# A decoder trunk's attention units: the value products one unit later, on one Trainium2 core

## The chip, the cores and the metric

The kernel runs on one core of one Trainium2 chip. The metric is the device time of one execution in microseconds (us), lower is better. Engines are named as in the profile: PE multiplies matrices (PEld loads its weights), DVE, ACT and POOL work on vectors, SP issues most DMAs. Each engine takes its instructions in the order of its own queue and waits at the head of the queue for what the instruction needs.

## The reference, cut to what matters

```python
u = x * (1 + scale) + shift                  # x: (2048, 1024)
q, k, v, a_gate, p_in, p_gate, m_a, m_p = split(u @ w_in)
# 16 query heads of 64, 2 key heads; blocks of 128 queries see the 256 keys of their own
# block and of the one before, within a window of 128
logits = qb @ kb.T * 64 ** -0.5 + bias       # masked by window
probs = softmax(concat([logits, sink], -1))[..., :-1]
a = (probs @ vb) * silu(a_gate)
p = (pool(p_in) @ w_mix * pool_scale) * silu(p_gate)
y = (sigmoid(m_a) * (a @ w_attn_proj) + sigmoid(m_p) * (p @ w_pool_proj)) @ w_out * (1 + gate)
x = layer_norm(alpha * x + y)
```

All of it is computed in fp32 accuracy: a matrix product is three products of high and low parts (`mm3`), so operands are split into a rounded copy and a rest (`low`, a subtraction).

## The kernel before

The 2048 rows are worked on in two halves of 1024 (`s` = 0, 1). For each half there are two phases, the gates' ring and the attention, and a last phase mixes both halves.

**The gates' ring** (`gate_quads`, `ring`, `back`) computes keys, values, gates and the first four query tiles. It works through groups of two pairs of weight tiles (`Quad`); one group, the last but one, has a single pair. `back` multiplies the group in five products a pair; `ask` puts off the load of a pair of the next group (`load`, issued on SP) by one tick and its first sum on POOL (`sum1`) by three. A tick is one product of twelve matmuls. SP's loads there are not held in program order: the layer that records the program may place them elsewhere in SP's queue.

**The attention** (`attention`) runs 64 units in each half and a few more that drain it. Unit `n` stands for two heads and one block of 128 queries. Its steps are spread over several units, so that in the loop's pass `n` the engines work on the units `n`, `n-1`, `n-2` and `n-3`:

- scores of unit `n` on PE (`score_mms`: four matmuls, tile `lg`); on DVE the bias is added and the row's bound taken, one instruction for each head (tiles `L`, `nm`); on ACT the exponential with its row sum (`L`, `sm`), again one for each head;
- of unit `n-1` on DVE the reciprocal of the sums (`sm`), on ACT the scaling of the first head's `L` by it, on DVE that of the second head's (a `tensor_scalar`);
- of unit `n-2` on PE four transposes (`turn_mms`, tile `pt`), on ACT the rounded copy `pth`, on DVE the rest `ptl`, then on PE the four value products (`value_mms`, tile `pv`, from `pth` and `ptl`);
- of unit `n-3` on ACT the copy of the lower half of `pv` (`o2`, shown as `o<-pv`), and on DVE two additions of `o2` and the upper half of `pv` into `o` (shown as `o<-pv,o`).

`pt`, `pv`, `pth` and `ptl` have one buffer each; `lg` has two, `L` three. All engines' instructions of this loop, the value products included, are kept in the order in which they are written. In each pass PE also runs 9 or 12 matmuls of another projection (`project`, shown as `mm<-set_..`), and for some passes ACT and DVE have more to do at the end of the pass: they split a tile of queries (`take_q`, tile `qs`: two instructions on ACT, then two on DVE), ACT copies a pool input (`vb`), DVE ends a pool difference (`pool_diff`, tile `nxt`). POOL adds pool sums and multiplies by gates.

In the pass before the change the additions of `n-3` stand on DVE behind the reciprocal and ahead of the two bias instructions, and PE's value products of `n-2` stand last.

Of the kernel before, what the change touches and what calls it, by code (L numbers as in the profile page):

```python
# [12 lines left out]
F32 = mybir.dt.float32  # L13
F32R = mybir.dt.float32r
AF = mybir.ActivationFunctionType
ALU = mybir.AluOpType
# [3 lines left out]
P = 128  # L20
# [3 lines left out]
CH = 512  # L24
NCH = S // CH
NB = CH // P
HEADS = 16
HD = 64
# [31 lines left out]
def kernel(  # L60
# [22 lines left out]
    nc = tc.nc  # L83
# [48 lines left out]
    def low(engine, dst, src, hi):  # L132
        engine.tensor_tensor(dst, src, as32(hi), ALU.subtract)  # L133
# [228 lines left out]

    def back(ph, grp, opened, nxt, own, tick, b22_first=False):
        st = []
        for q, (a, b, c, w, *copy) in zip(grp, opened):
            p5 = ph.p("p5")
            if w is None:
                c = bank("lg")
                nc.scalar.copy(c, a)
                nc.scalar.copy(p5, b)  # L370
                w = pair_split(ph, q.second())[::-1]
                q.late()
                product(c, w[1], "T2")
            else:
                u2 = copy[0] if copy else ph.p("u2")
                if not copy:
                    nc.scalar.copy(u2, a)
                if c is None:
                    c = bank("lg")
                    product(c, w[1], "T2", True)  # L380
                nc.vector.tensor_tensor(c, c, u2, ALU.add)
                nc.scalar.copy(p5, b)
            tick()
            nc.vector.tensor_tensor(b, c, p5, ALU.add)
            if not copy:
                product(a, w[0], "B21")
            tick()
            q.consume(ph, 0, 0, a)
            st.append((q, b, c, p5))
        w = {}  # L390

        def ask(q):

            defer(1, lambda: q.load(ph, own, sp if b22_first else nc.sync, None))
            defer(3, lambda: q.sum1(nc.gpsimd))

        def third(x):
            w[x] = pair_split(ph, st[x][0].third())[::-1]
            if x < len(nxt):
                ask(nxt[x])  # L400

        def with_t3(x):
            q, b, c, p5 = st[x]
            product(c, w[x][1], "T3")
            tick()
            nc.vector.tensor_tensor(p5, c, p5, ALU.add)
            q.consume(ph, 1, 1, p5)

        def with_b22(x):
            q, b, c, p5 = st[x]  # L410
            product(b, w[x][0], "B22")
            tick()
            q.consume(ph, 0, 1, b)

        if b22_first:
            for x in range(len(st)):
                third(x)
                with_b22(x)
            for x in range(len(st)):
                with_t3(x)  # L420
        else:
            for x in range(len(st)):
                third(x)
                with_t3(x)
                with_b22(x)
        for q in nxt[len(st) :]:
            ask(q)
        for q, b, c, p5 in st:
            w = half_split(ph, q.a22)
            product(c, w, "T4")  # L430
            tick()
            q.consume(ph, 1, 0, c)
# [29 lines left out]
    def defer(ticks, f):  # L462
        due.append((now[0] + ticks, len(due), f))
# [272 lines left out]
    def attention(ph, s, q0, nxt):  # L736
# [91 lines left out]
        def score_mms(j, b, q, qs):  # L828
            k0 = P if s == 0 and b == 0 else 0
            lg = bank("lg").rearrange("p (h k) -> p h k", h=2)  # L830
            for h in range(2):
                for hl in range(2):
                    mm(
                        lg[:, h, k0:],
                        qs[:, h, q * P : (q + 1) * P],
                        kk[:, j // 4, hl, b * P + k0 : (b + 2) * P],
                        start=hl == 0,
                        stop=hl == 1,
                    )
# [46 lines left out]
        bts = {0: bias_tile(0)}  # L886
        raw_q = {}
        parts, accs, sums = {}, {}, {}
        lgs, exps, Ls, pvs, outs, ags, pgs = {}, {}, {}, {}, {}, {}, {}
        opened = []  # L890
        act.activation(warm, mhalf, AF.Exp)

# [32 lines left out]
        for n in range(N + 5):  # L925
# [1 line left out]
            if n == 0:  # L927
                project(n)
            if n < N:
                lgs[n] = score_mms(j, n % U, b, qs[j, t])  # L930
            pt = None
            if n - 2 in Ls:
                L, k0 = Ls.pop(n - 2)
                pt = turn_mms(L, k0)
            if n - 1 in exps:
                sm = exps[n - 1][2]
                dve.reciprocal(sm, sm)
            if n - 3 in pvs:
                pv = pvs.pop(n - 3)
                jj, tt, bb = (n - 3) // U, (n - 3) // NB % 2, (n - 3) % NB  # L940
                if bb == 0:
                    outs[jj, tt] = tp.tile([P, CH], F32, tag="o", bufs=2, name="o")
                if bb == 1:
                    ags[jj, tt] = ld("ag", gates_d["ag"][s, jj, tt])
                o2 = tp.tile([HD, 2, P], F32, tag="o2", bufs=2, name="o2")
                act.copy(o2, pv[HD:])
                for h in range(2):
                    dve.tensor_tensor(
                        outs[jj, tt][h * HD : (h + 1) * HD, bb * P : (bb + 1) * P], pv[0:HD, h, :], o2[:, h, :], ALU.add
                    )  # L950
            if n - 1 in exps:
                E, e0, sm = exps[n - 1]
                act.activation(E[:, 0, e0:256], E[:, 0, e0:256], AF.Copy, scale=sm[:, 0:1])
            if pt is not None:
                h0 = k0 // P
                pth = tp.tile([P, 2, 2, P], F32R, tag="pth", bufs=1, name="pth")
                ptl = tp.tile([P, 2, 2, P], F32R, tag="ptl", bufs=1, name="ptl")
                act.copy(pth[:, h0:], pt[:, h0:])
            if n < N:
                lg, c0 = lgs.pop(n)  # L960
                L = tp.tile([P, 2, 260], F32, tag="L", bufs=3, name="L")
                nm = tp.tile([P, 2], F32, tag="nm", bufs=4, name="nm")
                sm = tp.tile([P, 2], F32, tag="sm", bufs=4, name="sm")
                act.copy(L[:, :, 256], nsink[:, 2 * j : 2 * j + 2])
# [19 lines left out]
                exps[n] = (L, c0, sm)  # L984
            if pt is not None:
                low(dve, ptl[:, h0:], pt[:, h0:], pth[:, h0:])
            if n - 1 in exps:
                E, e0, sm = exps.pop(n - 1)
                dve.tensor_scalar(E[:, 1, e0:256], E[:, 1, e0:256], sm[:, 1:2], None, ALU.mult)
                Ls[n - 1] = (E, e0)  # L990
            if 0 < n < 60:
                project(n)
            elif n >= 60:
                fill_one(n)
            if pt is not None:
                pvs[n - 2] = value_mms((n - 2) // U, (n - 2) % U, k0, pth, ptl)


            for w in range(1, len(order)):
# [546 lines left out]
```

## Time and profile before

| what | us |
|---|---|
| median of 3 runs (lowest, highest) | 1816.47 (1813.97, 1816.5) |
| the profiled execution's own time | 1815.8 |
| its span, first to last instruction | 1814.0 |
| first attention, units 0 to 63 begin | 455 to 704 |
| second attention, units 0 to 63 begin | 1076 to 1331 |

The mean granted clock of PE is 0.986 of full speed. In rows of the timeline the first number is the start in us from the span's start, the second the duration in us; a bracket at the end gives the engine's idle time just before and what released it. All instructions of the attention stand at line 56 of the kernel, through which the ordered engines record, so they are told apart by tiles. `(x)` in a table of stretches is the count of instructions.

### The profile page before, as it was taken

The numbers are of one execution on the slowest core, as the hardware profiler recorded it, in microseconds if no ns is written. First come the engines' busy times: TensorE is split into PE (matmuls) and PEld (weight loads), VectorE is DVE, ScalarE is ACT, GpSimd is POOL, SyncE is SP. The second block draws the span as 40 slices with busy tenths as digits, with TensorE's granted clock in tenths as the row PEclk, the third lists the DMA queues.
The fourth block names the chain that finished last, engine by engine and source line by source line (L and its number), as shares of the span: only waits on it lengthen the run. The fifth ranks groups of instructions, "written<-read, shape, count | busy, mean of one in ns | idle before, by whom it ended". The sixth has DMA issues, their size and how long they took to land. (4 is left out here: it accounts for less than half of the span.)

```text
span 1814.0 us, 25046 instructions
## 1 busy us (share of the span) xinstructions
PE 1718.8 (95%) x8200; PEld 1426.4 (79%) x8200; DVE 1232.6 (68%) x2200; ACT 951.7 (52%) x1997; POOL 804.7 (44%) x628
## 2 busy tenths in 40 slices
PE   6899999999998998999999999899999999999997
PEld 5688878878777787888788888677888877888785
DVE  5977656434777887667755338878877675865777
ACT  4644444434877777545444447777854334423452
POOL 2154344521265557434424304644574662355542
PEclk9999999999999999999999999999999999999998
DMA  9375766762445447686776454534687675689432
GB/s 359 123 273 196 244 238 252 264 150 98 146 161 169 163 149 302 235 289 247 276 265 241 168 192 140 175 134 158 219 304 275 198 234 185 232 287 399 166 140 105
DMA packets 185010, 387.60 MB, mean 214 GB/s; under 512 B 19232, under 2 KB 39728, under 8 KB 184880
## 3 DMA queue, kind: packets, MB, share of 16 engines
q1 hardware_dynamic: 178240, 370.22, 58.8%
q0 software_dynamic: 3552, 11.56, 1.6%
q10 hardware_dynamic: 3088, 4.23, 0.8%
q8 instruction: 65, 1.06, 0.2%
q14 instruction: 65, 0.53, 0.1%
HBM read 247.49 MB, written 141.59 MB: 214 GB/s over the span
## 5 line engine op out<-in xcount | busy, mean ns | idle before, releaser
L56 PE MATMUL mm<-set_B,w_set 128*128 128x512 f32 x3024 | 757.2, 397 | 11.8 <-DVE w_set L133 7.0
L56 PEld LDWEIGHTS mm<-set_B,w_set 128*128 128x128 f32 x3024 | 567.3, 190 | 131.8 <-DVE w_set L133 9.6
L56 PE MATMUL lg<-set_T,w_set 128*128 128x512 f32 x2232 | 542.6, 394 | 18.6 <-DVE w_set L133 10.3
L56 PEld LDWEIGHTS lg<-set_T,w_set 128*128 128x128 f32 x2232 | 419.6, 189 | 114.7 <-DVE w_set L133 14.9
L133 DVE TENSOR_TENSOR w_set<-W,w_set 128x1024 fp32r<-128x1024 f32 x174 | 237.4, 1364 | 230.2 <-ACT w_set L326 214.9
L326 ACT CAST w_set<-W 128x1024 fp32r<-128x1024 f32 x174 | 182.5, 1049 | 282.1 <-PE mm L56 220.1
L56 PE MATMUL mm<-set_T,w_set 128*128 128x512 f32 x1008 | 252.7, 395 | 0.0
L56 PEld LDWEIGHTS mm<-set_T,w_set 128*128 128x128 f32 x1008 | 188.8, 190 | 38.9 <-DVE nxt L56 0.2
L295 POOL TENSOR_TENSOR W<-W,A 128x512 f32<-128x512 f32 x60 | 85.3, 1422 | 267.3 <-DMA W<-in_win_dram 65.1
L304 POOL TENSOR_TENSOR W<-W 128x512 f32<-128x512 f32 x60 | 84.3, 1406 | 187.9 <-DVE w_set L133 177.8
L299 POOL TENSOR_TENSOR W<-W 128x512 f32<-128x512 f32 x60 | 95.9, 1599 | 97.3 <-DVE w_set L133 88.2
L56 ACT ACTIVATE L<-L,nm 128x257 f32<-128x257 f32 (+1 forms) x256 | 127.0, 498 | 12.0 <-DVE nm L56 6.8
L56 DVE TENSOR_TENSOR o<-pv,o 64x128 f32<-64x128 f32 x256 | 71.9, 281 | 66.2 <-ACT o L56 63.7
L56 DVE CUSTOM_DVE_ANT_0 L<-lg,bt,nsink 128x256 f32<-128x256 f32 (+1 forms) x256 | 111.5, 473 | 6.4 <-DMA bt<-e_rep 2.4
L300 POOL TENSOR_TENSOR W<-W 128x512 f32<-128x512 f32 x60 | 94.8, 1579 | 45.7 <-DMA W<-in_win_dram 31.1
L56 POOL TENSOR_TENSOR nxt<-vb 128x512 f32<-128x512 f32 (+3 forms) x32 | 35.1, 1097 | 158.7 <-ACT vb L56 85.6
L56 ACT ACTIVATE L<-L,sm 128x256 f32<-128x256 f32 (+1 forms) x128 | 64.3, 502 | 50.5 <-DVE sm L56 49.8
L56 DVE TENSOR_TENSOR ptl<-pt,pth 128x512 fp32r<-128x512 f32 (+1 forms) x128 | 85.6, 669 | 3.2 <-ACT pth L56 3.0
L56 PE MATMUL pv<-ptl,vv 128*128 128x256 f32 x248 | 71.0, 305 | 16.9 <-DVE ptl L56 16.5
L56 PE MATMUL pv<-pth,vv 128*128 128x256 f32 x248 | 70.6, 297 | 16.4 <-ACT pth L56 16.0
L56 DVE TENSOR_TENSOR k_lo<-spare,k_hi 128x512 fp32r<-128x512 f32 x61 | 61.7, 1016 | 29.3 <-ACT k_hi L56 8.1
L56 PE MATMUL lg<-kk,qs 128*128 128x256 f32 (+1 forms) x512 | 81.4, 282 | 0.0
(218 smaller groups left out, 2319.4 us busy)
## 6 DMA issues: line engine op xcount, KB each, us to landing
W<-in_win_dram SPq DMA_DIRECT2D x46, 512.0 KB, 5.0
w_set<-wmix_d SPq DMA_DIRECT2D x28, 512.0 KB, 4.8
W<-in_win_dram SPq DMA_DIRECT2D x38, 256.0 KB, 3.0
A<-in_win_dram SPq DMA_DIRECT2D x38, 256.0 KB, 4.9
ag_d<-sig SPq DMA_DIRECT2D x32, 256.0 KB, 3.2
pg_d<-sig SPq DMA_DIRECT2D x32, 256.0 KB, 3.6
ma_d<-sig SPq DMA_DIRECT2D x32, 256.0 KB, 4.2
mp_d<-sig SPq DMA_DIRECT2D x32, 256.0 KB, 3.5
```

The lines of the kernel that those rows point to most:

```text
L56: return lambda *args, **kw: self.tc.keep_in_program_order(op(*args, **kw))
L133: engine.tensor_tensor(dst, src, as32(hi), ALU.subtract)
L295: e.tensor_tensor(self.w[:, 1, :], self.w[:, 2, :], self.a22, ALU.add)
L299: e.tensor_tensor(x[:, 1, :], x[:, 1, :], x[:, 0, :], ALU.subtract)
L300: e.tensor_tensor(x[:, 2, :], x[:, 0, :], x[:, 2, :], ALU.subtract)
L304: e.tensor_tensor(x[:, 3, :], x[:, 3, :], x[:, 1, :], ALU.subtract)
L326: a.copy(by_two(hi), raw)
```

## The change

In the loop over `n`, `value_mms` of unit `n-2` at the end of the pass becomes `value_mms` of unit `n-3` right behind the scores and ahead of the transposes (`turned` keeps `pth` and `ptl` of one unit until then). On ACT the copy of the sink (`L<-nsink`) and the scaling come ahead of the copy `o2`. On DVE the two additions move from the front of the pass to its end. In `back`, as many pairs of the next group as it has more than this group are asked for at the start instead of behind the products.

```diff
+        ahead = len(nxt) - len(grp)
+        for q in nxt[: max(ahead, 0)]:
+            ask(q)
...
-            if x < len(nxt):
-                ask(nxt[x])
+            if x + max(ahead, 0) < len(nxt):
+                ask(nxt[x + max(ahead, 0)])
...
-        for q in nxt[len(st) :]:
-            ask(q)
...
-            pt = None
+                lg, c0 = score_mms(j, n % U, b, qs[j, t])
+            pt = pv = None
+            if n - 3 in turned:
+                pv = value_mms((n - 3) // U, (n - 3) % U, *turned.pop(n - 3))
             if n - 2 in Ls:
                 L, k0 = Ls.pop(n - 2)
-                pt = turn_mms(L, k0)
+                pt, h0 = turn_mms(L, k0), k0 // P
+            if 0 < n < 60:
+                project(n)
+            elif n >= 60:
+                fill_one(n)
...
             if n - 1 in exps:
-                sm = exps[n - 1][2]
-                dve.reciprocal(sm, sm)
-            if n - 3 in pvs:
-                pv = pvs.pop(n - 3)
...
+                E, e0, r = exps[n - 1]
+                dve.reciprocal(r, r)
+                act.activation(E[:, 0, e0:256], E[:, 0, e0:256], AF.Copy, scale=r[:, 0:1])
+            if pv is not None:
                 o2 = tp.tile([HD, 2, P], F32, tag="o2", bufs=2, name="o2")
                 act.copy(o2, pv[HD:])
-                for h in range(2):
-                    dve.tensor_tensor(
-                        outs[jj, tt][h * HD : (h + 1) * HD, bb * P : (bb + 1) * P], pv[0:HD, h, :], o2[:, h, :], ALU.add
-                    )
...
-            if 0 < n < 60:
-                project(n)
-            elif n >= 60:
-                fill_one(n)
-            if pt is not None:
-                pvs[n - 2] = value_mms((n - 2) // U, (n - 2) % U, k0, pth, ptl)
+            if pv is not None:
...
+                for h in range(2):
+                    dve.tensor_tensor(
+                        outs[jj, tt][h * HD : (h + 1) * HD, bb * P : (bb + 1) * P], pv[0:HD, h, :], o2[:, h, :], ALU.add
+                    )
```

PE in the first attention, one pass; the numbers of the tiles tell the units apart (`pth_4526` and `ptl_4527` are of the transposes just before). Before:

```order
L56 MATMUL mm_4545<-set_B11_66,w_set_4279 128x512
L56 MATMUL pv_4552<-pth_4526,vv_3359 128x256
L56 MATMUL pv_4552<-ptl_4527,vv_3359 128x256
L56 MATMUL pv_4552<-pth_4526,vv_3359 128x256
L56 MATMUL pv_4552<-ptl_4527,vv_3359 128x256
L56 MATMUL lg_4569<-kk_3358,qs_4397 128x256 x4
L56 MATMUL pt_4574<-ident_69,L_4474 128x128 x4
L56 MATMUL mm_4545<-set_B11_66,w_set_4278 128x512 x2
```

and now, at the same place (`pt_4574` is the same unit's):

```order
L56 MATMUL mm_4525<-set_B11_66,w_set_4274 128x512
L56 MATMUL lg_4564<-kk_3358,qs_4392 128x256 x4
L56 MATMUL pv_4569<-pth_4540,vv_3359 128x256
L56 MATMUL pv_4569<-ptl_4541,vv_3359 128x256
L56 MATMUL pv_4569<-pth_4540,vv_3359 128x256
L56 MATMUL pv_4569<-ptl_4541,vv_3359 128x256
L56 MATMUL pt_4574<-ident_69,L_4474 128x128 x4
L56 MATMUL mm_4525<-set_B11_66,w_set_4273 128x512 x2
```

The value products stand behind the next unit's scores, and between them and the transposes there is nothing else.

DVE in the first attention, the pass of unit 15, from the reciprocal to the next pass's reciprocal. Before:

```order
L56 RECIPROCAL sm<-sm 128x2
L56 TENSOR_TENSOR o<-pv,o_4310 64x128 x2
L56 ISA L,nm<-lg,bt,nsink 128x256
L56 ISA nm 128x1
L56 ISA L,nm<-lg,bt,nsink 128x256
L56 ISA nm 128x1
L56 TENSOR_TENSOR ptl<-pt,pth 128x512
L56 TENSOR_SCALAR L<-L,sm 128x256
L56 RECIPROCAL sm<-sm 128x2
```

and now:

```order
L56 RECIPROCAL sm<-sm 128x2
L56 ISA L,nm<-lg,bt,nsink 128x256
L56 ISA nm 128x1
L56 ISA L,nm<-lg,bt,nsink 128x256
L56 ISA nm 128x1
L56 TENSOR_TENSOR ptl<-pt,pth 128x512
L56 TENSOR_SCALAR L<-L,sm 128x256
L56 TENSOR_TENSOR o<-pv,o_4323 64x128 x2
L56 RECIPROCAL sm<-sm 128x2
```

The two additions, the last readers of `pv`, are now the last of the pass.

ACT in the first attention, one pass. Before:

```order
L56 COPY o_4194<-pv 64x256
L56 ACTIVATE L<-L,sm 128x256
L56 CAST pth<-pt 128x512
L56 COPY L<-nsink 128x2
L56 ACTIVATE L,sm<-L,nm 128x257 x2
```

and now:

```order
L56 COPY L<-nsink 128x2
L56 ACTIVATE L<-L,sm 128x256
L56 COPY o_4208<-pv 64x256
L56 CAST pth<-pt 128x512
L56 ACTIVATE L,sm<-L,nm 128x257 x2
```

The scaling, which needs DVE's reciprocal, stood between `o2` and `pth` and now stands ahead of both.

In the gates' rings no instruction of any engine stands elsewhere: the rows of PE, DVE, ACT, POOL and SP up to the first attention, and those between the first attention's last loads and the second attention, are the same in both kernels but for the numbers in the tiles' names. In the attention some loads on SP stand a few rows earlier or later (the gate tile `ag` ahead of the weights `w_set`, for one), and one sum on POOL at line 299 one row later.

More of the change, by code (lines that the diff above doesn't have):

```diff
@@ L364, in back, with ask @@
         st = []
+        def ask(q):
+            defer(1, lambda: q.load(ph, own, sp if b22_first else nc.sync, None))
+            defer(3, lambda: q.sum1(nc.gpsimd))
+        ahead = len(nxt) - len(grp)
+        for q in nxt[: max(ahead, 0)]:
+            ask(q)
         for q, (a, b, c, w, *copy) in zip(grp, opened):
@@ L390, in back @@
         w = {}
-        def ask(q):
-            defer(1, lambda: q.load(ph, own, sp if b22_first else nc.sync, None))
-            defer(3, lambda: q.sum1(nc.gpsimd))
         def third(x):
             w[x] = pair_split(ph, st[x][0].third())[::-1]
-            if x < len(nxt):
-                ask(nxt[x])
+            if x + max(ahead, 0) < len(nxt):
+                ask(nxt[x + max(ahead, 0)])
         def with_t3(x):
@@ L888, in attention @@
         parts, accs, sums = {}, {}, {}
-        lgs, exps, Ls, pvs, outs, ags, pgs = {}, {}, {}, {}, {}, {}, {}
+        exps, Ls, turned, outs, ags, pgs = {}, {}, {}, {}, {}, {}
         opened = []
@@ L929, in attention @@
             if n < N:
-                lgs[n] = score_mms(j, n % U, b, qs[j, t])
-            pt = None
+                lg, c0 = score_mms(j, n % U, b, qs[j, t])
+            pt = pv = None
+            if n - 3 in turned:
+                pv = value_mms((n - 3) // U, (n - 3) % U, *turned.pop(n - 3))
             if n - 2 in Ls:
                 L, k0 = Ls.pop(n - 2)
-                pt = turn_mms(L, k0)
-            if n - 1 in exps:
-                sm = exps[n - 1][2]
-                dve.reciprocal(sm, sm)
-            if n - 3 in pvs:
-                pv = pvs.pop(n - 3)
[L940 to L944, printed above, removed]
+                pt, h0 = turn_mms(L, k0), k0 // P
[3 more added lines that the diff above has]
+                fill_one(n)
+            if n < N:
+                L = tp.tile([P, 2, 260], F32, tag="L", bufs=3, name="L")
+                nm = tp.tile([P, 2], F32, tag="nm", bufs=4, name="nm")
+                sm = tp.tile([P, 2], F32, tag="sm", bufs=4, name="sm")
+                act.copy(L[:, :, 256], nsink[:, 2 * j : 2 * j + 2])
+            if n - 1 in exps:
+                E, e0, r = exps[n - 1]
+                dve.reciprocal(r, r)
+                act.activation(E[:, 0, e0:256], E[:, 0, e0:256], AF.Copy, scale=r[:, 0:1])
+            if pv is not None:
                 o2 = tp.tile([HD, 2, P], F32, tag="o2", bufs=2, name="o2")
                 act.copy(o2, pv[HD:])
-                for h in range(2):
-                    dve.tensor_tensor(
-                        outs[jj, tt][h * HD : (h + 1) * HD, bb * P : (bb + 1) * P], pv[0:HD, h, :], o2[:, h, :], ALU.add
-                    )
-            if n - 1 in exps:
-                E, e0, sm = exps[n - 1]
-                act.activation(E[:, 0, e0:256], E[:, 0, e0:256], AF.Copy, scale=sm[:, 0:1])
             if pt is not None:
-                h0 = k0 // P
                 pth = tp.tile([P, 2, 2, P], F32R, tag="pth", bufs=1, name="pth")
@@ L959, in attention @@
             if n < N:
[L960 to L964, printed above, removed]
                 for h in range(2):
@@ L986, in attention @@
                 low(dve, ptl[:, h0:], pt[:, h0:], pth[:, h0:])
+                turned[n - 2] = k0, pth, ptl
             if n - 1 in exps:
-                E, e0, sm = exps.pop(n - 1)
-                dve.tensor_scalar(E[:, 1, e0:256], E[:, 1, e0:256], sm[:, 1:2], None, ALU.mult)
+                E, e0, r = exps.pop(n - 1)
+                dve.tensor_scalar(E[:, 1, e0:256], E[:, 1, e0:256], r[:, 1:2], None, ALU.mult)
                 Ls[n - 1] = (E, e0)
-            if 0 < n < 60:
-                project(n)
-            elif n >= 60:
-                fill_one(n)
-            if pt is not None:
-                pvs[n - 2] = value_mms((n - 2) // U, (n - 2) % U, k0, pth, ptl)
+            if pv is not None:
+                jj, tt, bb = (n - 3) // U, (n - 3) // NB % 2, (n - 3) % NB
+                if bb == 0:
+                    outs[jj, tt] = tp.tile([P, CH], F32, tag="o", bufs=2, name="o")
+                if bb == 1:
+                    ags[jj, tt] = ld("ag", gates_d["ag"][s, jj, tt])
+                for h in range(2):
+                    dve.tensor_tensor(
+                        outs[jj, tt][h * HD : (h + 1) * HD, bb * P : (bb + 1) * P], pv[0:HD, h, :], o2[:, h, :], ALU.add
+                    )
             for w in range(1, len(order)):
```

## The prediction

> **What bounds the kernel now.** I read the page first, then the stretches of the two attentions, the waits, and one smooth and one disturbed pass of the timeline.
>
> ```profile
> span 1814.0 us, 25046 instructions
> PE 1718.8 (95%) x8200; PEld 1426.4 (79%) x8200; DVE 1232.6 (68%) x2200; ACT 951.7 (52%) x1997; POOL 804.7 (44%) x628
> ```
>
> PE is busy for 95% of the span. The stretches show where it is not (us long, then busy us of PE, PEld, DVE, ACT and POOL):
>
> ```profile
> 455.00:710.00 255.00, 237.55 (x1334) 200.54 (x1333) 201.22 (x617) 194.54 (x593) 139.83 (x116) 0.99 0.50 171
> ...
> 1076.00:1336.00 260.00, 241.38 (x1366) 204.06 (x1365) 208.21 (x617) 198.58 (x593) 138.28 (x108) 0.99 0.49 169
> ```
>
> In each attention PE idles some 18 us of 255 to 260. The waits name the place, and a row of the page DVE's own wait there:
>
> ```profile
> PE pv L56 <- DVE ptl L56: 16.5, 35, 0.8
> PE pv L56 <- ACT pth L56: 16.0, 20, 2.8
> L56 DVE TENSOR_TENSOR o<-pv,o 64x128 f32<-64x128 f32 x256 | 71.9, 281 | 66.2 <-ACT o L56 63.7
> ```
>
> So 32.5 us of PE's wait stand ahead of the value products, for the copy and the rest made in the same pass. That is the wait that the change goes at. The question is what the value products wait for in their new place. A smooth pass (unit 14, from the scores at 504.23 to those at 507.70, with three DVE rows of the pass before):
>
> ```profile
> 502.78 0.68 DVE L56 TENSOR_TENSOR ptl<-pt,pth 128x512 fp32r<-128x512 f32 x1
> 503.39 0.34 DVE L56 TENSOR_SCALAR L<-L,sm 128x256 f32<-128x256 f32 x1
> 503.65 0.68 DVE L56 SCALAR_TENSOR_TENSOR nxt<-nxt,mm 128x512 f32<-128x512 f32 x1
> 503.73 0.28 PE L56 MATMUL pv<-pth,vv 128*128 128x256 f32 x1
> ...
> 504.23 0.63 PE L56 MATMUL lg<-kk,qs 128*128 128x256 f32 x4
> 504.70 0.60 PE L56 MATMUL pt<-ident,L 128*128 128x128 f32 x4
> 505.05 2.33 PE L56 MATMUL mm<-set_B,w_set 128*128 128x512 f32 x9
> 505.33 0.59 ACT L56 CAST pth<-pt 128x512 fp32r<-128x512 f32 x1
> 505.82 0.20 ACT L56 COPY L<-nsink 128x2 f32<-128x2 f32 x1
> 506.05 0.51 ACT L56 ACTIVATE L<-L,nm 128x257 f32<-128x257 f32 x1
> 507.70 0.64 PE L56 MATMUL lg<-kk,qs 128*128 128x256 f32 x4
> ```
>
> A pass with 9 large matmuls takes 3.47 us on PE with no wait; three more, at 2.33/9 = 0.26 us, add 0.7 to 0.8. From value products to scores it is 0.50 us, from scores to transposes 0.47, from there to `pth` 0.63. On DVE `ptl` occupies 0.61, the scaling 0.26 until the next starts.
>
> A disturbed pass (unit 44; the one before it splits a tile of queries):
>
> ```profile
> 626.40 0.37 ACT L56 COPY o<-pv 64x256 f32<-64x256 f32 x1 [0.30 <-PE pv L56]
> 626.67 0.51 ACT L56 ACTIVATE L<-L,sm 128x256 f32<-128x256 f32 x1
> ...
> 630.29 1.39 DVE L56 SCALAR_TENSOR_TENSOR qs<-mm,qs 64x512 fp32r<-64x512 f32 x2 [1.04 <-ACT qs L56]
> 631.69 0.17 DVE L56 RECIPROCAL sm<-sm 128x2 f32<-128x2 f32 x1
> 631.95 0.51 ACT L56 ACTIVATE L<-L,sm 128x256 f32<-128x256 f32 x1 [1.30 <-DVE sm L56]
> 632.49 0.59 ACT L56 CAST pth<-pt 128x512 fp32r<-128x512 f32 x1
> 633.32 0.68 DVE L56 TENSOR_TENSOR ptl<-pt,pth 128x512 fp32r<-128x512 f32 x1
> 634.06 0.38 PE L56 MATMUL pv<-ptl,vv 128*128 128x256 f32 x1 [0.55 <-DVE ptl L56]
> 634.51 0.63 PE L56 MATMUL lg<-kk,qs 128*128 128x256 f32 x4
> ```
>
> The queries on DVE wait for both of ACT's instructions and put the reciprocal off; everything of the pass follows from it, and PE's next scores start 634.51 - 631.69 = 2.82 us after it. A pass of 3.47 us therefore bears a reciprocal up to 0.65 us after its own start; in the smooth pass it could have started at 503.65, 0.58 before, so DVE has about 1.2 us to spare.
>
> **The change: the new loop.** `pv` has one buffer, and the two additions that read it last now end DVE's pass. So the next value products wait for them, and the transposes, behind them on PE, wait as well; behind the transposes come `pth`, `ptl`, the scaling and the additions. This closes a loop of one pass: value products to transposes 0.50, to `pth` 0.63, `pth` and its handoff 0.59 + 0.05, `ptl` 0.61, scaling 0.26, two additions 2 x 0.28 = 0.56, handoff 0.06 (633.32 + 0.68 to 634.06): 3.26 us against PE's 3.47. It fits by 0.2 us, as long as every step is at its best. Before, the additions stood at DVE's front and no such loop held the transposes.
>
> *Step 1, the second head's scaling.* It is often not at its best:
>
> ```profile
> L56 DVE TENSOR_SCALAR L<-L,sm 128x256 f32<-128x256 f32 x120 | 74.4, 620 | 0.0
> ...
> L56 DVE TENSOR_SCALAR L<-L,sm x128: 274/346/2497, 458.8 to 1337.2; 128x256 f32<-128x256 f32 x120, 128x128 f32<-128x128 f32 x8
> ...
> 528.92 1.30 POOL L56 TENSOR_TENSOR p<-p,p 128x512 f32<-128x512 f32 x1
> ...
> 529.53 0.84 DVE L56 TENSOR_SCALAR L<-L,sm 128x256 f32<-128x256 f32 x1
> ```
>
> The median is 346 ns, the mean 620: 74.4 - 120 x 0.346 = 32.9 us of excess, on at most half of the 120. In the row shown it ends at 530.37, just behind POOL's at 530.22. Of a slow one all but the 0.2 us of room now reaches PE: with some 45 of them (my estimate under that bound) 32.9 - 45 x 0.2 = 24 us. Some fall in passes with twelve matmuls, which have 0.7 us more, or where PE waits anyway; I take two thirds, 16. Before, 1.2 us of room hid all but the longest, about 2 us. Net +14, between 0 (all covered elsewhere) and +24.
>
> *Step 2, the query tiles.*
>
> ```profile
> L56 DVE SCALAR_TENSOR_TENSOR qs<-mm,qs 64x512 fp32r<-64x512 f32 x40 | 27.6, 689 | 26.4 <-ACT qs L56 26.0
> ...
> L56 DVE SCALAR_TENSOR_TENSOR qs<-raw_q,qs 64x512 fp32r<-64x512 f32 x24 | 26.0, 1082 | 5.5 <-ACT qs L56 5.1
> ...
> L56 DVE SCALAR_TENSOR_TENSOR nxt<-nxt,mm 128x512 f32<-128x512 f32 x32 | 21.8, 681 | 1.8 <-POOL nxt L56 1.4
> ```
>
> 64/2 = 32 tiles, of which 28 are split inside the loops. After such a tile the chain is now: reciprocal to scaling 0.26, scaling 0.54 (631.95 to 632.49), `o2` 0.27 (626.40 to 626.67), then `pth` 0.64, `ptl` 0.61, scaling 0.26, additions 0.56, handoff 0.06: 3.20 us to the value products. These stand 0.47 behind the scores, so in the old measure it is 2.73 against 2.82: the same wait for the same late reciprocal. The value products have a pass more, but their producers stand in the same queues. And the reciprocal comes later: with the value products ahead of the transposes ACT's exponentials start 0.50 later, less 0.23 for the sink's copy that left the way (505.82 to 506.05), so 0.27, and the queries follow the exponentials. Net +0.2 each, +6; bounds -2 (only the shorter chain) and +13 (twice the shift).
>
> *Step 3, pool differences.* 32 of them hold DVE 0.60 us each (681 ns less overlap). Additions now end 0.47 + 0.50 + 0.63 + 0.64 + 0.61 + 0.26 + 0.56 = 3.67 us into a pass, 0.20 into the next; the reciprocal may be as late as 3.47 + 0.47 - 3.20 = 0.74. The room is 0.54, so each costs 0.06 to 0.1: +3, bounds 0 and +10 where one meets a slow scaling.
>
> *Step 4, what falls away.* Twenty-eight query waits of about 0.28 + 0.55 us each explain 23 of the 32.5 us; the other 9 are short waits behind ACT's casts. I let half go: -4, bounds -9 and 0.
>
> *Step 5, the clock.*
>
> ```profile
> 512.75 0.38 PE L56 MATMUL pv<-pth,vv 128*128 128x256 f32 x1 [1.89 <-ACT pth L56]
> ...
> 512.50:515.50 3.00, 2.33 (x10) 2.13 (x11) 1.78 (x7) 2.91 (x11) 0.00 (x0) 0.68 0.97 363
> ```
>
> Behind a wait of 1.9 us the granted clock was 0.68 in this stretch. Waits of that length stay about as many: +1, bounds 0 and +5. The Trainium skill (TensorE: Matmul & The Clock Gate, What's actually happening) has the clock fall after an idle window of about 3.4 us; by that rule alone waits this short would be free and the term 0. The trace disagrees.
>
> *Step 6, the ring.* No row of any queue there moves, so 0. Were the loads really asked sooner, the most to be had is the one wait in such a group:
>
> ```profile
> 394.71 5.49 PE L56 MATMUL lg<-set_T,w_set 128*128 128x512 f32 x12 [4.07 <-ACT lg L369]
> ```
>
> so -4 to 0. The loads that SP issues a few rows earlier or later in the attention go to tiles with two passes to spare; 0.
>
> The sum: 14 + 6 + 3 - 4 + 1 = +20 us. The profiled execution took 1815.8, 1.8 over its span and 0.7 under the median: 1815.8 + 20 = 1836. The bounds add up to -15 and +53.
>
> The Trainium skill (Perfetto Trace Analysis, Matmuls) says that independent groups should rotate through PSUM banks so that emptying one overlaps the next group's matmuls. `pv` has one bank, and the change moves its emptying behind everything else; the rule speaks against it, as steps 1 and 2 do.
>
> **The rivals.**
> - *The spare pass works* (faster). If DVE ends its additions before PE's value products in nearly all passes, the 9 us of short waits go, and DVE, freed of its 63.7 us of waiting for `o2`, catches up earlier behind query tiles and saves perhaps a quarter of their 23: 1815.8 - 15 = 1801. It decides at the 0.2 us of room: fewer than about ten slow scalings would have to meet it. For it: DVE has 201 busy us in 255. Against: 32.9 us of excess sit in the loop. Chance 0.10.
> - *Nothing measurable* (gains and losses cancel, 1816): 0.05.
> - *The loop is over PE's pass.* If its five handoffs took 0.06 us more each, 0.3 in all, it would be 3.56 against 3.47: 0.1 us in each of some 100 passes with nine matmuls and 0.1 more on 45 slow scalings, +14: 1850. For it: no trace of before shows this chain in one piece. Chance 0.15.
> - *POOL is late too.* The product of `o` with its gate waits for the last addition, which now ends 3.67 us into its pass and so at most 3.1 us later, 32 times; POOL's pool sums queue behind it and DVE's difference behind those. A third of this on the way to PE: 32 x 3.1 / 3 = 33 at worst, I take 10: 1846. Against: POOL is busy 140 of 255 us. Chance 0.10.
> - The forecast itself: 0.60.
>
> **How the numbers follow.** The likeliest is 1836. Faster takes 0.10, no change (within 0.2%, 3.6 us, about what a measurement of this kernel can tell) 0.05, slower 0.60 + 0.15 + 0.10 = 0.85. The range leaves out the faster case and part of no change below, and the worst of the loop case above: 1817 to 1858.
>
> **What would show it.** After the change PE's waits at `pv` should name DVE's `o` in place of `ptl` and `pth`, with more than 40 us in all; passes behind a slow scaling should be longer by its excess less 0.2; the 2.8 us from a late reciprocal to the next scores should stay. The gates' rings should keep their times. A smooth pass over 3.5 us means the loop case; waits at `pv` under 20 us in all mean that I am wrong, and then the room I gave DVE's pass is the step to look at.

## The result, and the profile after

The changed kernel takes 1845.01 us (median of 4 runs, 1843.13 to 1847.13), the kernel before beside it 1815.22: a ratio of 1.0165 (95% interval 1.0147 to 1.0182), 30 us slower. The forecast was 1836 within 1817 to 1858.

The head of the page of after, the waits of PE, and two groups of instructions (busy us, mean ns of one, idle us before them and what ended it):

```profile
span 1845.3 us, 25040 instructions
PE 1721.8 (93%) x8200; PEld 1435.9 (78%) x8200; DVE 1229.7 (67%) x2200; ACT 943.5 (51%) x1997; POOL 810.1 (44%) x628
```

```profile
PE pv L56 <- DVE o L56: 47.0, 51, 2.4
PE pv L56 <- ACT vb L56: 14.9, 6, 3.2
```

```profile
L56 DVE TENSOR_TENSOR ptl<-pt,pth 128x512 fp32r<-128x512 f32 x120 | 83.0, 692 | 104.9 <-ACT pth L56 104.9
L56 DVE TENSOR_TENSOR o<-pv,o 64x128 f32<-64x128 f32 x256 | 71.4, 279 | 1.7
```

PE no longer waits at the value products for `ptl` and `pth` (32.5 us before) but for DVE's additions into `o`, the last readers of `pv`: 47.0 us, and 14.9 more where the profile names `vb`. That is the same wait: in the longest of them, shown below under the clock, the additions end at 515.71 + 0.57 = 516.28 and the products begin at 516.42, and in the trace the products begin 0.15 us behind the end of the additions after every one of these waits, whatever name stands there. In all 61.9 us, 29.4 more than before. (Such rows count from the modelled end of the matmul before; what the change costs is read below from the lengths of the stretches, which need no model.) DVE's idle time has moved as well: it no longer waits for `o2` ahead of the additions (66.2 us before, 1.7 now) but for `pth` ahead of the rests (104.9 now, 3.1 before).

The two attentions, stretches from the first unit's scores to those of unit 63 (us long, then busy us of PE, PEld, DVE, ACT, POOL, the granted clock, the DMA share, GB/s). Before:

```profile
454.90:704.30 249.40, 231.95 (x1304) 196.09 (x1303) 195.93 (x603) 191.30 (x583) 134.28 (x112) 0.99 0.49 165
1075.80:1330.60 254.80, 236.18 (x1335) 199.50 (x1334) 203.32 (x604) 195.34 (x583) 133.04 (x105) 0.99 0.48 163
```

and after:

```profile
454.90:717.00 262.10, 233.68 (x1299) 201.69 (x1298) 192.13 (x601) 186.84 (x583) 134.90 (x113) 0.96 0.46 158
1091.30:1361.40 270.10, 237.13 (x1332) 204.47 (x1331) 197.73 (x601) 190.96 (x583) 133.91 (x105) 0.97 0.45 154
```

The attentions are 12.7 and 15.3 us longer: 28.0 of the span's 31.3. The first one begins at the same time, so the first ring kept its time; from the first attention to the second it is 374.3 us after and 371.5 before. The granted clock fell from 0.99 to 0.96 and 0.97. No group of instructions on DVE, ACT or POOL carries the loss: in each attention DVE and ACT are busy for 3.8 to 5.6 us less than before, and POOL for at most 0.9 us more. It is waiting, and slower matmuls behind the waits.

A late pass of after, the counterpart of the disturbed pass before (timeline; unit 45, the pass before it splits a tile of queries):

```profile
638.84 1.39 DVE L56 SCALAR_TENSOR_TENSOR qs<-mm,qs 64x512 fp32r<-64x512 f32 x2 [0.64 <-ACT qs L56]
640.25 0.17 DVE L56 RECIPROCAL sm<-sm 128x2 f32<-128x2 f32 x1
640.51 0.51 ACT L56 ACTIVATE L<-L,sm 128x256 f32<-128x256 f32 x1 [1.48 <-DVE sm L56]
640.92 0.35 ACT L56 COPY o<-pv 64x256 f32<-64x256 f32 x1
641.30 0.59 ACT L56 CAST pth<-pt 128x512 fp32r<-128x512 f32 x1
641.49 0.63 PE L56 MATMUL lg<-kk,qs 128*128 128x256 f32 x4
641.92 0.69 DVE L56 TENSOR_TENSOR ptl<-pt,pth 128x512 fp32r<-128x512 f32 x1 [0.58 <-ACT pth L56]
642.53 0.34 DVE L56 TENSOR_SCALAR L<-L,sm 128x256 f32<-128x256 f32 x1
642.79 0.57 DVE L56 TENSOR_TENSOR o<-pv,o 64x128 f32<-64x128 f32 x2
643.51 0.36 PE L56 MATMUL pv<-pth,vv 128*128 128x256 f32 x1 [1.39 <-DVE o L56]
...
646.58 0.63 PE L56 MATMUL lg<-kk,qs 128*128 128x256 f32 x4
```

This is the chain of the prediction in one piece: reciprocal, scaling, `o2`, `pth`, `ptl`, scaling, additions, value products: 643.51 - 640.25 = 3.26 us, where 3.20 was worked out (the last handoff, from 643.36 to 643.51, is 0.15 us in place of 0.06, and the steps on ACT are a little shorter). The pass lasts 646.58 - 641.49 = 5.09 us against 3.47 for a smooth one.

A pass behind a slow scaling in after (unit 48):

```profile
653.23 2.41 POOL L56 TENSOR_TENSOR w_set<-W,w_set 128x1024 fp32r<-128x1024 f32 x1
...
654.51 1.27 DVE L56 TENSOR_SCALAR L<-L,sm 128x256 f32<-128x256 f32 x1
...
655.71 0.57 DVE L56 TENSOR_TENSOR o<-pv,o 64x128 f32<-64x128 f32 x2
...
656.43 0.36 PE L56 MATMUL pv<-pth,vv 128*128 128x256 f32 x1 [0.75 <-DVE o L56]
```

The additions begin 655.71 - 654.51 = 1.20 us behind the scaling's start, 0.94 later than the usual 0.26; PE waits 0.75. So all but 0.2 us of the excess reaches PE, as step 1 had it; in nine of the twelve passes where neither a query tile nor a pool difference stands ahead of the slow scaling, the wait is the excess less 0.2 to 0.3 us. The scaling ends at 655.78, POOL's instruction at 655.64. That is the rule in the trace: each of after's 50 scalings of more than 0.45 us ends 0.08 to 0.15 us behind the end of an instruction of POOL, as do all 53 of the kernel before.

The clock behind a long wait in after (unit 16, then a stretch in the order of the columns above):

```profile
515.71 0.57 DVE L56 TENSOR_TENSOR o<-pv,o 64x128 f32<-64x128 f32 x2
...
516.42 0.55 PE L56 MATMUL pv<-pth,vv 128*128 128x256 f32 x1 [3.21 <-ACT vb L56]
...
518.12 4.19 PE L56 MATMUL mm<-set_B,w_set 128*128 128x512 f32 x9
```

```profile
518.20:521.20 3.00, 3.00 (x9) 2.38 (x8) 2.08 (x3) 2.65 (x8) 2.78 (x3) 0.50 0.22 84
```

Behind a wait of 3.21 us PE runs at 0.50 of its clock, and nine large matmuls take 4.19 us instead of 2.33. Counted over both attentions from the starts of the large matmuls, such slow stretches cost 12.8 us in nine passes of after and 3.2 us in three of before. The profiled execution of after is the slowest of its four, with a mean granted clock of 0.981; two of the others have 0.985, so the usual cost may be somewhat smaller.

### The profile page after: what moved, and what is told of

Its sections match the earlier page's. It is cut to its first block, busy times and chain, and to the rows that moved or that the text cites. A ratio compares the mean times of both kernels' runs of the same rounds, so it can differ in the third digit from the quotient of the medians.

```text
span 1845.3 us, 25040 instructions
## 1 busy us (share of the span) xinstructions
PE 1721.8 (93%) x8200; PEld 1435.9 (78%) x8200; DVE 1229.7 (67%) x2200; ACT 943.5 (51%) x1997; POOL 810.1 (44%) x628
## 5 line engine op out<-in xcount | busy, mean ns | idle before, releaser
L56 PE MATMUL mm<-set_B,w_set 128*128 128x512 f32 x3024 | 766.0, 401 | 14.0 <-DVE w_set L133 6.4
L56 PEld LDWEIGHTS pv<-pth,vv 128*128 128x128 f32 x248 | 47.1, 190 | 74.1 <-ACT L L56 33.9
L56 PEld LDWEIGHTS lg<-kk,qs 128*128 128x128 f32 x512 | 78.6, 190 | 11.4 <-DVE nm L56 1.0
```

What stands on the lines that cost most here:

```text
L56: return lambda *args, **kw: self.tc.keep_in_program_order(op(*args, **kw))
```

## The experiments

All ratios are to the kernel before, run on the same chip; its medians there were 1816.6 to 1820.5 us.

**e1_ring: the ring's part alone.** The kernel before with the new order of asking in `back`.

```diff
-            if x < len(nxt):
-                ask(nxt[x])
+            if x + max(ahead, 0) < len(nxt):
+                ask(nxt[x + max(ahead, 0)])
```

> The kernel before with the ring's part of the change alone. My account (the loads' rows do not move): the time of before, 1815 within 3 us, and no row of a view differs by more than the spread. Rival (part of the 30 us comes from the ring): 1818 or more, with a wait longer than 4.1 us in a group with one pair.

Measured 1819.72 us (1812.56 to 1826.26, 10 runs), ratio 1.0011 (0.9992 to 1.003). The ring's part does nothing that can be measured.

**e2_values: the value products alone.** The kernel before with the value products one pass later; the additions stay at DVE's front.

```diff
+            if n - 3 in turned:
+                pvs[n - 3] = value_mms((n - 3) // U, (n - 3) % U, *turned.pop(n - 3))
...
-                pvs[n - 2] = value_mms((n - 2) // U, (n - 2) % U, k0, pth, ptl)
+                turned[n - 2] = k0, pth, ptl
```

> The kernel before with PE's part alone: the value products one pass later, behind the scores; DVE's additions stay at the front of its pass, ACT's order stays. My account: the products then wait for DVE's rest ptl of the pass before, and the additions for o2, which now follows products 1 us into the pass; value products, o2, additions, two bias instructions and ptl make a loop of 0.64 + 0.42 + 0.60 + 0.81 + 0.69 + 0.06 = 3.2 us, which fits into 3.47, and query tiles cost what they did: 1815 to 1825. It would say that the additions at the end of DVE's pass, not the later products, cost the 30 us. Rival (the spare pass for the products is worth its 32.5 us of waits): 1800 or less. Rival (the later transposes alone cost it): 1840 or more.

Measured 1819.08 us, ratio 1.001 (0.9993 to 1.0027). Its waits at the value products:

```profile
PE pv L56 <- DVE ptl L56: 14.4, 31, 0.8
PE pv L56 <- ACT pth L56: 13.0, 13, 2.4
```

A pass more for the producers brings 5 us of shorter waits at this place and nothing in the time: the products still wait for the same late `pth` and `ptl`.

**e3_adds: the additions alone.** The kernel before with DVE's additions at the end of the pass.

```diff
-                for h in range(2):
-                    dve.tensor_tensor(outs[jj, tt][...], pv[0:HD, h, :], o2[:, h, :], ALU.add)
...
+            if pv is not None:
+                for h in range(2):
+                    dve.tensor_tensor(outs[jj, tt][...], pv[0:HD, h, :], o2[:, h, :], ALU.add)
```

> The kernel before with DVE's part alone: the additions at the end of DVE's pass, the value products where they were. My account: the products, with one pv, wait in the same pass for scores 0.47, transposes 0.63, pth 0.64, ptl 0.61, scaling 0.26, additions 0.56, handoff 0.06 = 3.23 us against their place at 2.97: +0.26 in some 100 passes, slow scalings in full (25 us and more) and 0.8 more behind each of 28 query tiles: 1865, between 1850 and 1885, with DVE's o as releaser of PE's pv. Rival (additions at the end are harmless, the order on PE costs): 1815 to 1825.

Measured 1864.3 us, ratio 1.0256 (1.0234 to 1.0279).

```profile
PE pv L56 <- DVE o L56: 72.4, 86, 2.7
```

The move of two instructions on DVE, which take 0.56 us of a pass wherever they stand, costs 46 us by itself. After has the later value products and ACT's new order as well and is some 17 to 19 us faster than this, so these two don't cause the loss; they give a part of it back. ACT's new order was not run alone, so which of the two does it is not shown.

**e4_mid: after, with the additions ahead of `ptl`.**

```diff
+            if pv is not None:
+                ...
+                    dve.tensor_tensor(outs[jj, tt][...], pv[0:HD, h, :], o2[:, h, :], ALU.add)
             if pt is not None:
                 low(dve, ptl[:, h0:], pt[:, h0:], pth[:, h0:])
...
-            if pv is not None:
-                ...
```

> The changed kernel with the two additions ahead of ptl instead of behind the scaling; they fill DVE's wait for pth (104.9 us in all after the change). My account: pv is free 0.9 us and more earlier, the loop value products, transposes, pth, ptl is 0.50 + 0.63 + 0.64 + 0.69 + 0.06 = 2.5 us, slow scalings have 0.8 us of room before the next transposes, and behind a query tile the chain is 2.46 us to the value products instead of 3.2: not only the 30 us go but also part of before's waits at the value products: 1803, between 1790 and 1812, PE's waits at pv below 25 us. Rival (the value products and transposes themselves, not the additions, hold PE): 1835 to 1850.

Measured 1806.74 us (1797.13 to 1811.09), ratio 0.9928 (0.9898 to 0.9959): the change turns from 30 us slower to 11 us faster.

```profile
PE pv L56 <- DVE o L56: 14.6, 14, 2.8
...
PE pv L56 <- DVE ptl L56: 6.0, 22, 0.3
L56 DVE TENSOR_SCALAR L<-L,sm 128x256 f32<-128x256 f32 x120 | 71.7, 598 | 0.0
```

The scalings are as slow as ever (598 ns in the mean), but the additions no longer stand behind them. ACT's new order and the ring's are those of after, so neither makes after slow. With e3 this shows the cause from both sides: what costs is that the last readers of `pv` stand behind the rest and the scaling.

**e5_odd: after, with the second head's scaling over 257 columns.** The idea was that an odd width would keep DVE's scaling from waiting for POOL.

```diff
-                dve.tensor_scalar(E[:, 1, e0:256], E[:, 1, e0:256], r[:, 1:2], None, ALU.mult)
+                dve.tensor_scalar(E[:, 1, e0:257], E[:, 1, e0:257], r[:, 1:2], None, ALU.mult)
```

> The changed kernel, with the second head's scaling on DVE over 257 columns instead of 256 (the last is the sink's, which nobody reads afterwards). My account of step 1 (an even-width scaling waits behind a running POOL instruction, and the loop then passes its excess on to PE; the Trainium skill, SBUF — State Buffer, SBUF: two separate sides, has such an instruction of DVE and one of POOL exclude each other for their whole length): an odd width takes the plain rate, near the bias instruction's 481 ns for 256 elements, and waits for nobody; the mean falls from 558 to about 480, the longest from 1545 to under 700; the loop, 0.13 longer, still fits 3.47; of the 25 us of excess some 7 come back net: 1838, between 1833 and 1843. Rival (the long ones have another cause): the longest stay over 1000 ns and the time at 1845.

Measured 1846.81 us, ratio 1.0158 (1.0136 to 1.018): a miss.

```profile
L56 DVE TENSOR_SCALAR L<-L,sm x128: 279/349/1552, 458.4 to 1372.6; 128x257 f32<-128x257 f32 x120, 128x129 f32<-128x129 f32 x8
```

Median 349 and longest 1552 ns (346 and 1545 in after): the odd width changes neither. The premise, that an odd width lets the scaling go past POOL, was wrong: each of the 51 scalings of more than 0.45 us ends 0.08 to 0.16 us behind an instruction of POOL here too. So the run doesn't test what the slow scalings cost.

**e6_pool: after, without a part of POOL's work.** The pool sums after the first and five subtractions of the queries' and keys' operands are left out, so the output is not the reference's.

```diff
             while k < w:
+                if k > 1:
+                    break
...
-            pool.tensor_tensor(t1, x, t1, ALU.subtract)
```

> The changed kernel with part of POOL's work in the attention left out: of each pool window's chain of sums all but the first, and the five subtractions that build the stored sums of gated tiles (so the output is not the reference's). My account: fewer running POOL instructions for the scaling to wait behind: POOL's busy time in the two attentions falls from 269 to near 170 us, the scaling's excess over its 346 ns median from 25 us to some 12, and the time by two thirds of that, to 1837, between 1830 and 1842. Rival (POOL is no part of it): 1845 within 3.

Measured 1824.73 us, ratio 1.0041 (1.0024 to 1.0059): 20 us less than after, where 8 were expected.

```profile
L56 DVE TENSOR_SCALAR L<-L,sm 128x256 f32<-128x256 f32 x120 | 53.7, 448 | 0.0
L56 DVE SCALAR_TENSOR_TENSOR qs<-raw_q,qs 64x512 fp32r<-64x512 f32 x24 | 20.3, 848 | 1.0
```

The scalings lost half of their excess, as expected, but the rests of the raw queries on DVE are shorter as well (848 ns; 1139 in after, 1082 in the kernel before). Those cost the kernel before too, so a control was needed. What POOL work was left shows the mechanism at its clearest (timeline of e6):

```profile
597.81 2.36 POOL L56 TENSOR_TENSOR w_set<-W,w_set 128x1024 fp32r<-128x1024 f32 x1
...
598.15 2.17 DVE L56 TENSOR_SCALAR L<-L,sm 128x256 f32<-128x256 f32 x1
...
600.24 0.57 DVE L56 TENSOR_TENSOR o<-pv,o 64x128 f32<-64x128 f32 x2
...
600.96 0.36 PE L56 MATMUL pv<-pth,vv 128*128 128x256 f32 x1 [2.29 <-DVE o L56]
```

This scaling starts while POOL works and ends with POOL (600.32 and 600.17), and PE waits 2.29 us for it. The Trainium skill (SBUF — State Buffer, SBUF: two separate sides) has DVE and GpSimd share a pair of ports as an exclusive lock for a whole instruction; these rows agree.

**e9_pool_control: the kernel before without the same POOL work.**

> The kernel before, with the same POOL work left out as in e6_pool (the later pool sums and the five subtractions on POOL; output not the reference's). It tells how much of e6's 20 us belongs to the change. If the slow scalings cost only through the change's loop: 1812 to 1818, no change against the kernel before, with scalings' excess falling from 33 to about 15 us at no gain. If the left-out work, among it the raw query rests that wait behind POOL on DVE, also costs the kernel before: 1800 to 1810, and then only 20 minus that difference belongs to the change. I expect the second, about 1808, that is 8 of the 20 us common to both.

Measured 1805.09 us, ratio 0.9919 (0.9891 to 0.9947): 15 us less. The waits for `pth` fell from 16.0 to 9.4 us, and the raw queries' rests from 1082 to 815 ns:

```profile
PE pv L56 <- ACT pth L56: 9.4, 19, 1.9
L56 DVE SCALAR_TENSOR_TENSOR qs<-raw_q,qs 64x512 fp32r<-64x512 f32 x24 | 19.6, 815 | 6.2 <-ACT qs L56 5.8
```

So most of e6's gain is nothing of the change's own. Without this POOL work the change costs 1.0041/0.9919 = 1.0123, about 22 us in place of 30. By the intervals of the three ratios this difference of 8 us is known to about 7.

**e7_defer: after, with DVE's half of the query split put off to the next pass,** behind the additions of that pass and its bias instructions. Some of the tiles that are read from memory are also begun a pass earlier.

```diff
-            for h in range(2):
-                ...
-                dve.scalar_tensor_tensor(qs[...], acc[...], -0.125, ..., ALU.mult, ALU.subtract)
+            def rest(): ...
+            if put_off:
+                rests.append(rest)
...
+            while rests:
+                rests.pop(0)()
...
-                    at = 8 * m - 2 + 2 * st
+                    at = 8 * m - (2 if st else 3) + 2 * st
```

> The changed kernel with DVE's half of a query split put off by one pass (behind the additions of the next pass, so that it does not wait for ACT's half; tiles that are read from memory are begun one pass earlier where the time is short). My account of step 2: the reciprocal then starts 1.5 us into the next pass instead of 2.2 and more, with room to 0.74; a query pass takes 4.2 us instead of 5.1, 28 of them, and the clock falls less often: 1820, between 1810 and 1832. Rival (slow scalings and pool differences alone carry the 30 us): 1840 or more.

Measured 1834.19 us, ratio 1.0097 (1.0074 to 1.0121): 11 us less than after, half of what was expected.

```profile
PE pv L56 <- DVE o L56: 37.8, 52, 2.5
PE pv L56 <- ACT vb L56: 11.4, 5, 3.2
```

The waits for the additions stay at 49.2 of 61.9 us. The rests that were put off no longer wait for ACT, but they still stand ahead of the next reciprocal: in one such pass they take 1.38 us from 1273.78 on, the reciprocal starts at 1275.19, 1.61 us behind its scores where the forecast allows 0.74, and PE waits 0.83 us in the pass behind.

**e10_defer_control: the kernel before with the same deferral.**

> The kernel before, with DVE's half of the query split put off to the next pass. If query tiles cost as much in the kernel before as my step 2 says (about 0.8 us of wait for each of 28): 1800 to 1806, some 13 us faster, and then e7_defer's 11 us against after are nothing of the change's own. If the deferral helps after only (waits that the change itself lengthened): 1812 to 1818. I expect the first, 1803.

Measured 1799.78 us, ratio 0.9897 (0.987 to 0.9924): 20 us faster than the kernel before, more than the deferral brings after.

```profile
PE pv L56 <- ACT pth L56: 5.9, 9, 1.7
```

The waits for `pth` fell from 16.0 to 5.9 us. So the query tiles cost the kernel before nearly what step 4 said (28 times some 0.8 us, 23 in all), and the change does not cost less where their rests are put off: 1.0097/0.9897 = 1.0202.

**e11_turn and e12_turn_defer: after, with the transposes ahead of the value products;** e12 with the deferral too.

```diff
-            if n - 3 in turned:
-                pv = value_mms((n - 3) // U, (n - 3) % U, *turned.pop(n - 3))
             if n - 2 in Ls:
                 ...
                 pt, h0 = turn_mms(L, k0), k0 // P
+            if n - 3 in turned:
+                pv = value_mms((n - 3) // U, (n - 3) % U, *turned.pop(n - 3))
```

> After, with the transposes ahead of the value products, so that on PE the transposes no longer stand behind the wait for the additions. The loop is then value products 0.50, handoff 0.1, copy 0.64, rest 0.61, scaling 0.26, additions 0.56, handoff 0.06: 2.73 us against 3.47, a room of 0.7 in place of 0.2; and since the value products stand 1.07 behind the scores in place of 0.47, a late reciprocal puts the next scores off by 0.6 less. If the loop is the cause: slow scalings lose about 10 us, the 28 query tiles about 15, sum 1820 (1810 to 1830), with waits at the value products under 45 us. If it is only the additions' late place on DVE, whatever stands behind them on PE: no gain, 1840 to 1850.

> e11_turn with DVE's half of the query split put off to the next pass as in e7_defer. If the loop is the cause and query tiles and slow scalings are what meet it: 1805 (1797 to 1815), below the kernel before. If the loop isn't the cause: like e7_defer, 1830 to 1838.

Measured 1842.54 us (1.0152, 1.0123 to 1.0181) and 1827.46 us (1.006, 1.0036 to 1.0084): both miss; e11 lies where its rival put it, at no gain (1840 to 1850). The waits of e11 say why. They have moved from the value products, where 1.0 us is left for the additions, to the transposes:

```profile
PE pt L56 <- DVE ptl L56: 32.9, 27, 2.7
PE pt L56 <- DVE L L56: 10.8, 27, 0.8
```

`pt` has one buffer as `pv` has; its last reader is DVE's rest `ptl`, and half of the transposes need DVE's scaling. The forecast let the transposes start freely. A late pass of e11 (units 44 and 45):

```profile
637.75 0.17 DVE L56 RECIPROCAL sm<-sm 128x2 f32<-128x2 f32 x1
...
640.16 0.81 PE L56 MATMUL pt<-ident,L 128*128 128x128 f32 x4 [0.94 <-DVE ptl L56]
...
641.00 0.36 PE L56 MATMUL pv<-pth,vv 128*128 128x256 f32 x1
...
642.13 0.59 ACT L56 CAST pth<-pt 128x512 fp32r<-128x512 f32 x1
```

From the late reciprocal to the value products it is still 3.25 us. The transposes, now ahead, wait for the rest and the scaling, and when they are done the additions are done too. So PE waits for DVE's late chain as before, only at an earlier link. A second thing was left out of the 0.7 us of room: on ACT `o2` stands ahead of `pth` and waits for the value products even where the transposes don't, so `pth` still comes 642.13 - 641.00 = 1.13 us behind them, as in the forecast's loop (0.50 + 0.63). How much of the miss belongs to each, and whether the transposes' place would matter with `o2` behind `pth`, was not tried.

**e8_mid_defer: both repairs, the additions ahead of `ptl` and the deferral, on after.**

> The additions ahead of ptl and DVE's half of the query split put off by one pass. My account: the reciprocal behind a query split comes 0.9 us into its pass, with room to 1.5, so tiles split from PSUM cost nothing and those read from memory about 0.5 each; PE's waits at pv fall from 20 us to 6 or less and the clock stays up: 1790, between 1780 and 1800. Rival (the deferred half only moves the wait, to PE's scores or to the scaling): 1803 to 1810.

Measured 1792.27 us (1791.42 to 1797.45), ratio 0.9864 (0.9845 to 0.9883): faster than both kernels, 25 us under the one before. Against e10 on the same scale it is 0.9864/0.9897 = 0.9967: the rest of the change, with the additions ahead of `ptl`, may be worth about 6 us here, but the two intervals overlap. PE's waits at the value products are down to 12.6 us, where 6 or less were expected:

```profile
PE pv L56 <- DVE o L56: 7.6, 8, 1.8
...
PE pv L56 <- DVE ptl L56: 5.0, 19, 0.3
```

## Why the prediction was right, and where its sum was off

The mechanism is the one forecast: the value products wait for the additions (e3 makes the loss alone, e4 takes it away alone), the late chain is 3.26 us for 3.20, a slow scaling reaches PE less 0.2 to 0.3 us, the ring does nothing (e1). The smooth pass stayed at 3.46 to 3.47 us, so the loop case is out. The time came out 9 us over the forecast, and one step accounts for about that much. (The upper bounds of the steps add up to +52, not +53.)

*Step 5, the clock, was mis-sized:* +1 (0 to +5) against 12.8 - 3.2 = +9.6 us in the profiled executions. It assumed that waits long enough to slow PE stay about as many. But the chain adds to passes that were already late: all nine slow stretches of after lie in the pass behind one that took 4.8 to 7.8 us in the kernel before. Six waits at `vb` alone make 14.9 us in after. By the Trainium skill's idle window of about 3.4 us (TensorE: Matmul & The Clock Gate, What's actually happening) none of them would have cost anything; the 0.50 behind 3.21 us disagrees, and a wait of 1.84 us (last section) more clearly.

*Steps 1 to 4* came to +19 in the forecast. Measured, without the slow matmuls, it is 28.0 - 9.6 = +18.4. That the sum agrees doesn't show that its terms do; it may be luck in part. For *step 1* (+14) the trace of after gives a bound. PE's waits at the value products come to 59.3 us in the two attentions; the smaller of the wait and of the excess of the scaling just ahead, added up over them, is 13.7 us, 7.3 of it in passes with neither a query tile nor a pool difference ahead. So +14 is at that bound, and a part of it may have been lost in the kernel before too. For *step 2* (+6) five clean passes behind a query tile went from 4.79-4.85 to 5.07-5.09 us, some +0.25 where +0.2 was forecast. What it is around the raw queries, whose rests take 1.1 us each in the kernel before, is not known. I grouped the 126 passes by whether, in the kernel before, DVE begins a query tile's rest in the pass or in the one ahead of it: 60 such passes lengthened by 12.7 us without the slow matmuls, the other 66 by 5.7. But the split hangs on how a tile is counted: by the first of its two rests alone the shares are 3.8 and 14.5 us, and with one pass more behind it about 15 and 3. So how the 18.4 us divide among steps 1, 2 and 3 stays open. By e6 and e9 about 8 us of the 30, known to about 7, go with the POOL work left out there, and by the slow matmuls (3.2 to 12.8 with it, 1.8 to 5.3 without) some 6 of these 8 are clock. How much of the rest hangs on POOL's remaining work, whose 2.36 us are shown in e6, stays open too: it was not taken away.

*Step 4* let half of the short waits go. e2 shows 5 us of shorter waits and no gain from them, which fits its small size.

*POOL late too* (the product of `o` with its gate): the waits of PE that grew name the additions, none a result of POOL's; no run took this case apart from the rest.

## What to carry to other kernels

A tile with one buffer closes a loop from its last reader to its next writer: when a producer is moved, look at where that last reader stands in its own engine's queue and put it ahead of everything that the writer doesn't need. Look at every such tile: in e11 the wait only moved from `pv` to `pt`. Two additions of 0.28 us were worth 46 us by their place alone (e3), and some 40 between after and e4. Cost a longer wait together with what the slower clock behind it adds.

## What the runs showed of the hardware

PE's clock fell behind waits that were shorter than I had allowed for, but not behind all of them. In after (timeline; the second unit follows the longer wait):

```profile
552.03 0.36 PE L56 MATMUL pv<-pth,vv 128*128 128x256 f32 x1 [1.84 <-DVE o L56]
...
552.93 3.89 PE L56 MATMUL mm<-set_B,w_set 128*128 128x512 f32 x9
```

```profile
482.33 0.36 PE L56 MATMUL pv<-pth,vv 128*128 128x256 f32 x1 [2.04 <-ACT vb L56]
...
483.23 2.33 PE L56 MATMUL mm<-set_B,w_set 128*128 128x512 f32 x9
```

A wait of 1.84 us was followed by nine matmuls in 3.89 us, one of 2.04 us by nine in 2.33. So the length of the wait alone doesn't decide it in this range; all five waits of 2.3 us or more in after's attentions were followed by slow matmuls. What else decides it stays open. The second surprise is e5's: a scaling on DVE over an odd number of columns kept the same 0.35 us, and was held behind POOL as long as one over an even number (at most 1552 and 1545 ns).
